# Weight parts interleaved element by element, paired activations, and streams read backward, in a float32 decoder layer on one core

## The chip, the cores and the metric

The kernel runs on one core of one Trainium2 chip. The metric is the device time of one execution in microseconds (us). Before the change it is 1109.9 us, the median of two runs (1109.86 and 1109.95). TensorE (PE in the profile) multiplies: it loads a 128 x 128 block (the stationary operand; the loads are shown as PEld) and streams columns past it (the moving operand). VectorE is DVE, ScalarE is ACT, GpSimd is POOL and SyncE is SP; SP issues the loads of weights.

## The reference

One decoder layer in float32, 256 tokens, width 2048. What matters here is its four weight products:

```
h = rms_norm(x, ln_mix_pre)
proj = h @ w_in                                   # 2048 x 5648
mixed = concat([attn, ssm]) @ w_out               # 2048 x 2048
x = x + rms_norm(mixed, ln_mix_post)
h = rms_norm(x, ln_ffn_pre)
u = causal_depthwise_conv(h @ w_ffn_up)           # 2048 x 11264
gate, up = split(u)
f = (gelu(gate, approximate=True) * up) @ w_ffn_down   # 5632 x 2048
x = x + rms_norm(f, ln_ffn_post)
```

Attention (8 heads) and the state-space mixer (16 heads) work on the 256 tokens between the first two products.

## The kernel before, in words

**Split operands.** Every operand of the four products is split into two parts, hi (the value rounded to fp32r) and lo (the rest). A product is hi·hi + lo·hi + hi·lo. Activations are split once; weights are split on the fly.

**Units of weights.** Weights come in units of 128 x 1024 elements (512 KB), in the order in which they are used: 88 of the input projection, 32 of the output projection, and twice 88 of the up and 44 of the down projection. `Weights.rounded` handles one unit: SP loads it into `raw` (L77), ACT writes `whi` (L78), DVE writes `wlo` (L79). `raw` has four slots. `whi` and `wlo` have four slots each, as separate tiles, and seven from the output projection on (`deepen`). Whenever TensorE has used a unit, `tick` fetches the next one for which there is a slot.

**Two forms of product.** In the *column* form (`cols_part`, L214 and L215; input projection in part, and up) the weights are stationary: a 128 x 128 slice of hi is loaded and both parts of the activations are streamed (512 columns), then the slice of lo is loaded and the hi activations are streamed (256 columns). A unit holds eight such pairs, and two units make one tile of 128 output columns. In the *row* form (`rows_part`, L278 to L280; the rest of the input projection, output and down) the activations are stationary and 512 columns of weights are streamed, three matmuls per slice, twelve per unit.

**The activations.** `hT` (input) and `mT` (output projection's input) hold the hi and lo parts of a slice of 128 rows one behind the other; `h2` (up) holds them as two planes; `gT` (down) is like `mT`. Up and down run in two halves of 22 slices each. An index `i` of the up loop makes one tile of the gate and one of the up branch; after it `cols_sum` adds the two column groups in PSUM (ACT L231, DVE L232), `conv_ffn` and `gated` apply the convolution, the gelu and the product, and `split_evac` (L201, L202) writes slice `i` of `gT`.

**What sets the order.** TensorE's order is that of the program; ACT's and DVE's are made by a scheduler from the program and its dependences, except around the second norm, where it is written by hand.

Of the kernel before, what the change touches and what calls it, by code (L numbers as in the profile page):

```python
# [19 lines left out]
P = 128  # L20
D = 2048
S = 256
# [18 lines left out]
LOE = UE + 2 * SHIFT  # L41
HOLD = 5
MORE = {"raw": 0, "whi": 3, "wlo": 3}
# [15 lines left out]
class Weights:  # L59

    def __init__(self, nc, pool, units):
        self.nc, self.pool, self.units = nc, pool, units
        self.fetched, self.ready, self.more, self.base, self.behind = 0, [], None, 0, 0

    def deepen(self, pool):

        self.more, self.base, self.behind = pool, self.fetched, MORE["whi"]

# [11 lines left out]
    def place(self, i, n, bufs, dtype):  # L82
        pool = self.pool
        if self.more and (i - self.base) % (bufs + MORE[n]) < MORE[n]:
            pool, bufs = self.more, MORE[n]
        wide = n == "wlo" and pool is self.pool
        return pool.tile([P, LOE if wide else UE], dtype, name=n, tag=n, bufs=bufs)
# [36 lines left out]
def decoder_layer(ctx, tc, x, xT, win, wdt, wout, wup, wdown, relb, vec, cols, mconv, fconv,  # L124
# [85 lines left out]
    def cols_part(ps, w, aT, k, j):  # L210

        s = tok(j)
        both, hi, c = wide_and_hi(aT, k)
        nc.tensor.matmul(ps, w[0][:, s], both, start=(k == 0), stop=False)  # L214
# [14 lines left out]
    def cols_sum(dst, ps):  # L229

        nc.scalar.copy(dst, ps[:, S:])  # L231
        nc.vector.tensor_tensor(dst, ps[:, :S], dst, op=ALU.add)  # L232
# [17 lines left out]
    def cols_tile(ps, aT):  # L250
        for u in range(2):
            w = ws.take()
            for j in range(8):
                cols_part(ps, w, aT, u * 8 + j, j)
# [57 lines left out]
    def units(w, a, n, shift=0):  # L312
        return [(w[i], shift) for i in range(a, a + n)]
# [4 lines left out]
                    for u in units(wup, half * 88, 88) + units(wdown, half * 44, 44)])  # L318
# [32 lines left out]
    def summands(aT):  # L351

        if len(aT.shape) == 4:
# [591 lines left out]
    gT = fp.tile([P, HALF, 2, S], F32R, name="gT")  # L945
# [5 lines left out]
    def summed(ps):  # L951
        u = fp.tile([P, S], F32, name="cfu", tag="cf", bufs=8)
        cols_sum(u, ps)
# [51 lines left out]
    def gated(i, ug, uu):  # L1005
# [5 lines left out]
        split_evac(gT, k, slice(0, S), cu)  # L1011
# [134 lines left out]
```

## Time and profile before

| | |
|---|---|
| median of two runs | 1109.9 us |
| profiled execution, first to last instruction | 1107.4 us |
| around it (median less span) | 2.5 us |
| mean granted TensorE clock | 0.998 |
| busy: PE / DVE / ACT | 99% / 71% / 53% |
| moved by DMA | 217.58 MB, mean 196 GB/s |

The page gives no time of its own for the profiled execution beside its span, so the 2.5 us are the median less the span. A busy PE is not a TensorE at its peak, since ends of matmuls are modelled; the pace at which matmuls start is what counts. In groups of instructions the last columns are the busy time, the mean of one in ns, the idle time of the engine before them, and what ended it. In rows by stage each engine has its busy time and, in brackets, its number of instructions.

### The profile page before, as it was taken

The numbers are of one execution on the slowest core, as the hardware profiler recorded it, in microseconds if no ns is written. First come the engines' busy times: TensorE is split into PE (matmuls) and PEld (weight loads), VectorE is DVE, ScalarE is ACT, GpSimd is POOL, SyncE is SP. The second block draws the span as 40 slices with busy tenths as digits, with TensorE's granted clock in tenths as the row PEclk, the third lists the DMA queues.
The fourth block names the chain that finished last, engine by engine and source line by source line (L and its number), as shares of the span: only waits on it lengthen the run. The fifth ranks groups of instructions, "written<-read, shape, count | busy, mean of one in ns | idle before, by whom it ended". The sixth has DMA issues, their size and how long they took to land.

```text
span 1107.4 us, 15791 instructions
## 1 busy us (share of the span) xinstructions
PE 1100.1 (99%) x5888; PEld 945.1 (85%) x5888; DVE 784.0 (71%) x1270; ACT 592.3 (53%) x914; POOL 15.5 (1%) x26
## 2 busy tenths in 40 slices
PE   9999999999999999999999999999999999999997
PEld 7888888888888988888888888888888888888886
DVE  6698976776566899878787644448787878765553
ACT  6666545545454586555555444345555555554441
POOL 0010000000000000000000000000000000000000
PEclk9999999999999999999999999999999999999999
DMA  8857555555687267665556665565566565666652
GB/s 297 298 187 262 186 154 167 177 172 168 217 298 245 96 216 242 192 189 190 191 188 189 194 195 190 192 194 188 191 189 191 189 192 190 189 201 219 200 158 76
DMA packets 61356, 217.58 MB, mean 196 GB/s; under 512 B 7200, under 2 KB 8624, under 8 KB 60384
## 3 DMA queue, kind: packets, MB, share of 16 engines
q1 hardware_dynamic: 59328, 207.64, 58.3%
q0 software_dynamic: 1664, 8.59, 2.3%
q8 instruction: 46, 0.75, 0.3%
q10 hardware_dynamic: 288, 0.35, 0.1%
q14 instruction: 30, 0.25, 0.1%
HBM read 214.44 MB, written 2.11 MB: 196 GB/s over the span
## 4 chain that ended last, share of the span: by engine, by line
PE 99%; DMA 0%; SPq 0%; ACT 0%; issue 0%; DVE 0%; POOLq 0%; ACTq 0%
PE pa L214 36%; PE pa L215 18%; PE pa L278 9%; PE pa L280 9%; PE pa L279 9%; PE ph L280 4%; PE ph L279 4%; PE ph L278 4%; PE pab L214 1%; PE pa L223 1%; PE pab L215 1%; PE py L604 1%; PE pa L226 0%; PE pq L223 0%; DMA raw<-in_win_dram 0%; PE lg L694 0%
## 5 line engine op out<-in xcount | busy, mean ns | idle before, releaser
L79 DVE TENSOR_TENSOR wlo<-raw,whi 128x1024 fp32r<-128x1024 f32 (+2 forms) x389 | 469.7, 1210 | 249.0 <-ACT whi L78 240.9
L78 ACT CAST whi<-raw 128x1024 fp32r<-128x1024 f32 (+2 forms) x389 | 403.7, 1040 | 415.5 <-PE pa L214 193.3
L214 PE MATMUL pa<-h,whi 128*128 128x512 f32 x1360 | 471.7, 394 | 0.0
L215 PE MATMUL pa<-h,wlo 128*128 128x256 f32 x1360 | 379.4, 279 | 0.0
L214 PEld LDWEIGHTS pa<-h,whi 128*128 128x128 f32 x1360 | 255.7, 188 | 57.7
L215 PEld LDWEIGHTS pa<-h,wlo 128*128 128x128 f32 x1360 | 255.5, 188 | 0.0
L214 PE MATMUL pa<-hT,whi 128*128 128x512 f32 x384 | 136.5, 397 | 0.0
L215 PE MATMUL pa<-hT,wlo 128*128 128x256 f32 x384 | 107.0, 281 | 0.0
L214 PEld LDWEIGHTS pa<-hT,whi 128*128 128x128 f32 x384 | 72.1, 188 | 15.2 <-issue 0.2
L962 DVE SCALAR_TENSOR_TENSOR cfc<-cfu,fcv,cfc 128x254 f32<-128x254 f32 (+1 forms) x176 | 83.5, 479 | 1.4
L215 PEld LDWEIGHTS pa<-hT,wlo 128*128 128x128 f32 x384 | 72.1, 189 | 0.6 <-issue 0.2
L278 PE MATMUL pa<-whi,gT 128*128 128x512 f32 x176 | 68.6, 390 | 0.0
L280 PE MATMUL pa<-whi,gT 128*128 128x512 f32 x176 | 68.5, 389 | 0.0
L278 PE MATMUL ph<-whi,gT 128*128 128x512 f32 x176 | 68.5, 389 | 0.0
L279 PE MATMUL pa<-wlo,gT 128*128 128x512 f32 x176 | 68.5, 389 | 0.0
L279 PE MATMUL ph<-wlo,gT 128*128 128x512 f32 x176 | 68.5, 389 | 0.0
L280 PE MATMUL ph<-whi,gT 128*128 128x512 f32 x176 | 68.5, 389 | 0.0
L960 ACT ACTIVATE cfc<-cfu,fcv 128x256 f32<-128x256 f32 x88 | 52.3, 598 | 1.3 <-DVE cfu L959 1.3
L278 PE MATMUL pa<-whi,hT 128*128 128x512 f32 x128 | 51.2, 400 | 0.0
L278 PE MATMUL pa<-whi,mT 128*128 128x512 f32 x128 | 50.3, 393 | 0.0
L280 PE MATMUL pa<-whi,hT 128*128 128x512 f32 x128 | 50.1, 392 | 0.0
L279 PE MATMUL pa<-wlo,hT 128*128 128x512 f32 x128 | 50.0, 391 | 0.0
(230 smaller groups left out, 1131.6 us busy)
## 6 DMA issues: line engine op xcount, KB each, us to landing
raw<-in_wup_dram SPq DMA_DIRECT2D x176, 512.0 KB, 3.7
raw<-in_wdown_dram SPq DMA_DIRECT2D x88, 512.0 KB, 3.6
raw<-in_win_dram SPq DMA_DIRECT2D x85, 512.0 KB, 3.6
raw<-in_wout_dram SPq DMA_DIRECT2D x32, 512.0 KB, 3.9
xsq<-in_x_dram SPq DMA_DIRECT2D x2, 1024.0 KB, 10.3
rows<-acd POOLq DMA_DIRECT2D x4, 512.0 KB, 8.9
xt<-in_x_dram POOLq DMA_DIRECT2D x2, 1024.0 KB, 6.7
xr<-in_xT_dram SPq DMA_DIRECT2D x6, 256.0 KB, 6.4
```

What stands on the lines that cost most here:

```text
L78: nc.scalar.copy(hi[:, s], raw[:, s])
L79: return lambda: nc.vector.tensor_tensor(lo[:, s], raw[:, s], f32(hi[:, s]), op=ALU.subtract)
L214: nc.tensor.matmul(ps, w[0][:, s], both, start=(k == 0), stop=False)
L215: end[0] = nc.tensor.matmul(ps[:, c], w[1][:, s], hi, start=False, stop=(k == KT - 1)).ins
L223: nc.tensor.matmul(both, w[0][:, s], aT[:, :, c:c + S][:, :, tok(t)], start=(t == 0 and k == 0), stop=False)
L278: nc.tensor.matmul(ps, a, w[0][:, s], start=(first and j == 0), stop=False)
L279: nc.tensor.matmul(ps, a, w[1][:, s], start=False, stop=False)
L280: end[0] = nc.tensor.matmul(ps, b, w[0][:, s], start=False, stop=(last and j == 1)).ins
L604: nc.tensor.matmul(py[:, i * 64:(i + 1) * 64], rows[:, t, g, i, :], xcs[t, g][:, i * 64:(i + 1) * 64], start=True, stop=True)
L960: nc.scalar.activation(c, u, AF.Identity, scale=wv[:, 2:3], bias=wv[:, 3:4])
L962: nc.vector.scalar_tensor_tensor(c[:, sh:], u[:, :S - sh], wv[:, 2 - sh:3 - sh], c[:, sh:], op0=ALU.mult, op1=ALU.add)
```

## The change

The two parts of a unit of weights now lie in one tile `wx`, with as many slots as before (four, and seven after `deepen`). A unit has one of three layouts. *plane*: hi in the first 1024 elements, lo in the next. *pair*: hi and lo alternate element by element, so that a slice of either is read and written at every second element. *plane-*: as plane, but each part is written backward, and the matmuls read it backward.

- Up: of the index `i`, `i % 4` in 0 and 1 is plane, 2 and 3 is pair. The start of a pair unit is shifted by 0, 16, 32 or 48 elements with `i // 4 % 4`, where the slot has room. For odd `i` above 1 the streamed `h2` is read backward (`back`), and `cols_sum` reads PSUM backward to put the columns right.
- Output projection: `mT` holds hi and lo element by element; they are the stationary operand.
- Down: weights in layout plane-, so the stream is read backward in both halves. `gT` stays in planes in the first half and is paired in the second.
- Input projection: layouts plane, and nothing is read backward.

```
-MORE = {"raw": 0, "whi": 3, "wlo": 3}
+MORE = 3
...
+    def place(self, i):
+        if self.more and (i - self.base) % (SPLB + MORE) < MORE:
+            return self.more.tile([P, 2 * UE], F32R, name="wx", tag="wx", bufs=MORE), 0
+        return self.pool.tile([P, 2 * UE + 2 * SHIFT], F32R, name="wx", tag="wx", bufs=SPLB), 1
...
-        raw = self.place(i, "raw", RAWB, F32)
-        hi, lo = (self.place(i, n, SPLB, F32R) for n in ("whi", "wlo"))
-        lo = lo[:, self.units[i][1]:][:, :UE]
+        raw = self.pool.tile([P, UE], F32, name="raw", tag="raw", bufs=RAWB)
+        w, room = self.place(i)
+        _, layout, shift = self.units[i]
+        if layout[:4] == "pair":
+            w = w[:, shift * room:][:, :2 * UE]
+            hi, lo = (w.rearrange("p (c z) -> p z c", z=2)[:, z, :] for z in range(2))
+        else:
+            hi, lo = w[:, :UE], w[:, UE + shift:][:, :UE]
+        if layout[-1] == "-":
+            hi, lo = hi[:, ::-1], lo[:, ::-1]
...
-    def cols_part(ps, w, aT, k, j):
+    def cols_part(ps, w, aT, k, j, back=False):
         s = tok(j)
         both, hi, c = wide_and_hi(aT, k)
+        if back:
+            both, hi = both[:, :, ::-1], hi[:, ::-1]
...
+    def cols_sum(dst, ps, back=False):
+        a, b = ps[:, S:], ps[:, :S]
+        if back:
+            a, b = a[:, ::-1], b[:, ::-1]
+        nc.scalar.copy(dst, a)
+        nc.vector.tensor_tensor(dst, b, dst, op=ALU.add)
...
+    layouts = ["plane", "plane", "pair", "pair"]
+    def up_units(i):
+        return units(wup, 4 * i, 4, 16 * (i // 4 % 4) if i % 4 > 1 else 0, layouts[i % 4])
...
-                    for u in units(wup, half * 88, 88) + units(wdown, half * 44, 44)])
+                    for u in [u for i in range(22 * half, 22 * half + 22) for u in up_units(i)]
+                    + units(wdown, half * 44, 44, 0, "plane-")])
...
-        mT = mx.tile([P, KT, 2, S], F32R, name="mT")
+        mT = mx.tile([P, KT, S, 2], F32R, name="mT")
+        mT = tuple(mT[:, :, :, c] for c in range(2))
...
-    gT = fp.tile([P, HALF, 2, S], F32R, name="gT")
+    gTs = fp.tile([P, HALF, 2 * S], F32R, name="gT")
+    gT = [tuple(gTs[:, :, c * S:(c + 1) * S] for c in range(2)),
+          tuple(gTs.rearrange("p k (s c) -> p k c s", c=2)[:, :, c, :] for c in range(2))]
...
+            back = i > 1 and i % 2 == 1
...
-                cols_tile(ps[-1], h2)
-            us = [summed(p) for p in ps]
+                cols_tile(ps[-1], h2, back)
+            us = [summed(p, back) for p in ps]
```

TensorE's instructions stand in the same order as before, and so do SP's and POOL's. ACT's and DVE's order moves, since the two parts share a tile. On DVE, in the first up stage, from the last step of one index to the splits of the next (`cfu` and `cfc` are an up tile and its convolution, `pa` is PSUM, L79 is the split of a unit), before:

```order
L202 TENSOR_TENSOR gT_3837<-cfc_4363,gT_3837 128x256
L232 TENSOR_TENSOR cfu_4461<-pa_4371,cfu_4461 128x256
L959 TENSOR_TENSOR cfu_4461<-cfu_4461,rb2_3841 128x256
L79 TENSOR_TENSOR wlo_4457<-raw_4455,whi_4456 128x1024
L79 TENSOR_TENSOR wlo_4500<-raw_4498,whi_4499 128x1024
L232 TENSOR_TENSOR cfu_4464<-pa_4416,cfu_4464 128x256
L962 SCALAR_TENSOR_TENSOR cfc_4467<-cfu_4461,fcv_3838,cfc_4467 128x255
L959 TENSOR_TENSOR cfu_4464<-cfu_4464,rb2_3841 128x256
L962 SCALAR_TENSOR_TENSOR cfc_4467<-cfu_4461,fcv_3838,cfc_4467 128x254
L79 TENSOR_TENSOR wlo_4522<-raw_4520,whi_4521 128x1024
```

The same place on DVE in the changed kernel (L81 is the split, L244 the sum out of PSUM, L982 and L985 the convolution):

```order
L209 TENSOR_TENSOR gT_3705<-cfc_4319,gT_3705 128x256
L244 TENSOR_TENSOR cfu_4413<-pa_4327,cfu_4413 128x256
L982 TENSOR_TENSOR cfu_4413<-cfu_4413,rb2_3709 128x256
L81 TENSOR_TENSOR wx_4409<-raw_4408,wx_4409 128x1024
L244 TENSOR_TENSOR cfu_4416<-pa_4370,cfu_4416 128x256
L982 TENSOR_TENSOR cfu_4416<-cfu_4416,rb2_3709 128x256
L985 SCALAR_TENSOR_TENSOR cfc_4419<-cfu_4413,fcv_3706,cfc_4419 128x255
L985 SCALAR_TENSOR_TENSOR cfc_4419<-cfu_4413,fcv_3706,cfc_4419 128x254
L81 TENSOR_TENSOR wx_4451<-raw_4450,wx_4451 128x1024
```

The sum of the second tile (L232, now L244) has moved ahead of the second split. On ACT, at the same place, before (L78 writes hi, L231 copies out of PSUM):

```order
L231 COPY cfu_4461<-pa_4371 128x256
L78 CAST whi_4456<-raw_4455 128x1024
L78 CAST whi_4499<-raw_4498 128x1024
L231 COPY cfu_4464<-pa_4416 128x256
L960 ACTIVATE cfc_4467<-cfu_4461,fcv_3838 128x256
L78 CAST whi_4521<-raw_4520 128x1024
```

And on ACT in the changed kernel (L80 writes hi, L243 copies out of PSUM):

```order
L243 COPY cfu_4413<-pa_4327 128x256
L80 CAST wx_4409<-raw_4408 128x1024
L243 COPY cfu_4416<-pa_4370 128x256
L983 ACTIVATE cfc_4419<-cfu_4413,fcv_3706 128x256
L80 CAST wx_4451<-raw_4450 128x1024
```

The copy of the second tile has moved ahead of the second cast.

More of the change, by code (lines that the diff above doesn't have):

```diff
@@ L67, in deepen @@
     def deepen(self, pool):
-        self.more, self.base, self.behind = pool, self.fetched, MORE["whi"]
+        self.more, self.base, self.behind = pool, self.fetched, MORE
     def split(self, raw, hi, lo, i, s):
@@ L80, in rounded @@
                                                op=ALU.subtract)
[L82 to L87, printed above, removed]
-    def tiles(self, i):
-        raw = self.place(i, "raw", RAWB, F32)
-        hi, lo = (self.place(i, n, SPLB, F32R) for n in ("whi", "wlo"))
-        lo = lo[:, self.units[i][1]:][:, :UE]
+    def place(self, i):
+        if self.more and (i - self.base) % (SPLB + MORE) < MORE:
+            return self.more.tile([P, 2 * UE], F32R, name="wx", tag="wx", bufs=MORE), 0
+        return self.pool.tile([P, 2 * UE + 2 * SHIFT], F32R, name="wx", tag="wx", bufs=SPLB), 1
+    def tiles(self, i):
+        raw = self.pool.tile([P, UE], F32, name="raw", tag="raw", bufs=RAWB)
[8 more added lines that the diff above has]
+            hi, lo = hi[:, ::-1], lo[:, ::-1]
         self.ready.append((hi, lo))
@@ L248, in tick, with cols_tile @@
                 fn(*args)
-    def cols_tile(ps, aT):
+    def cols_tile(ps, aT, back=False):
         for u in range(2):
@@ L253, in cols_tile @@
             for j in range(8):
-                cols_part(ps, w, aT, u * 8 + j, j)
+                cols_part(ps, w, aT, u * 8 + j, j, back)
             tick()
@@ L310, in rows_tail, with units @@
         rows_part(pss[t], tail[j], aT, kts[len(kts) - HOLD + j], t, False, j == HOLD - 1)
-    def units(w, a, n, shift=0):
-        return [(w[i], shift) for i in range(a, a + n)]
+    def units(w, a, n, shift=0, layout="plane"):
+        return [(w[i], layout, shift) for i in range(a, a + n)]
+    layouts = ["plane", "plane", "pair", "pair"]
+    def up_units(i):
+        return units(wup, 4 * i, 4, 16 * (i // 4 % 4) if i % 4 > 1 else 0, layouts[i % 4])
     ws = Weights(nc, wp, units(win, 0, 16, SHIFT) + units(win, 16, 16) + units(win, 32, 16, SHIFT)
@@ L351, in summands @@
     def summands(aT):
+        if isinstance(aT, tuple):
+            return aT
         if len(aT.shape) == 4:
@@ L949, in decoder_layer, with summed @@
     rb2 = pers.tile([P, S], F32, name="rb2", tag="rbc", bufs=1)
-    def summed(ps):
+    def summed(ps, back):
         u = fp.tile([P, S], F32, name="cfu", tag="cf", bufs=8)
-        cols_sum(u, ps)
+        cols_sum(u, ps, back)
         return u
@@ L1010, in gated @@
         nc.vector.tensor_tensor(cu, cg, cu, op=ALU.mult)
[L1011 removed]
+        split_evac(gT[i // HALF], k, slice(0, S), cu)
     held = []
@@ L1032, in decoder_layer @@
                 held.append([psum("ph") for _ in range(NT)])
-                rows_chunk(held[-1], gT, range(0, HALF, 2), last=False)
+                rows_chunk(held[-1], gT[half], range(0, HALF, 2), last=False)
             elif half == 1 and c == 2:
-                rows_chunk(held[0], gT, range(0, HALF, 2), first=False, done=fdone(1, c))
+                rows_chunk(held[0], gT[half], range(0, HALF, 2), first=False, done=fdone(1, c))
             elif half == 1 and c == 3:
@@ L1038, in decoder_layer @@
                 kts = range(0, HALF, 2)
-                tail = rows_to_tail(held[1], gT, kts, first=False)
+                tail = rows_to_tail(held[1], gT[half], kts, first=False)
                 for t in range(NT):
                     for j in range(HOLD):
-                        rows_tail(held[1], gT, kts, tail, t, j)
+                        rows_tail(held[1], gT[half], kts, tail, t, j)
                     fdone(1, 3)(t, held[1][t])
             else:
-                rows_chunk(chunk_psums(), gT, range(0, HALF, 2), done=fdone(half, c))
+                rows_chunk(chunk_psums(), gT[half], range(0, HALF, 2), done=fdone(half, c))
 def _cols_units(w):
```

4 lines of the change are left out of this document (removed).

## The prediction

> **What bounds the kernel now.** I read the page's busy times and its chain of waits first, then the stages one by one.
>
> ```profile
> PE 1100.1 (99%) x5888; PEld 945.1 (85%) x5888; DVE 784.0 (71%) x1270; ACT 592.3 (53%) x914; POOL 15.5 (1%) x26
> ...
> PE 99%; DMA 0%; SPq 0%; ACT 0%; issue 0%; DVE 0%; POOLq 0%; ACTq 0%
> PE pa L214 36%; PE pa L215 18%; PE pa L278 9%; PE pa L280 9%; PE pa L279 9%; PE ph L280 4%; PE ph L279 4%; PE ph L278 4%; PE pab L214 1%; PE pa L223 1%; PE pab L215 1%; PE py L604 1%; PE pa L226 0%; PE pq L223 0%; DMA raw<-in_win_dram 0%; PE lg L694 0%
> ```
>
> The chain that ends last is TensorE for 99% of the span; no other engine and no transfer has a whole percent of it. So the time is the number of matmuls times the pace at which TensorE starts them. Ends of matmuls are modelled (each is shown some 0.17 us longer than the step to the next), so I take the pace from counts in stages: the first up stage, the first down, the second up, the second down, and the output projection.
>
> ```profile
> core 0: us, PE busy (x) PEld busy (x) DVE busy (x) ACT busy (x) POOL busy (x), PEclk, DMA share, GB/s
> 390.00:610.00 220.00, 220.00 (x1271) 193.09 (x1270) 181.15 (x300) 135.30 (x215) 0.72 (x1) 1.00 0.62 199
> 625.00:725.00 100.00, 100.00 (x443) 82.86 (x442) 45.17 (x37) 40.73 (x41) 0.00 (x0) 1.00 0.61 194
> 760.00:970.00 210.00, 210.00 (x1213) 184.28 (x1212) 165.62 (x265) 122.11 (x190) 0.00 (x0) 1.00 0.60 189
> 985.00:1085.00 100.00, 100.00 (x442) 82.83 (x442) 51.53 (x53) 43.71 (x50) 0.00 (x0) 1.00 0.55 182
> 300.00:360.00 60.00, 60.00 (x267) 49.68 (x265) 40.26 (x47) 29.11 (x36) 0.00 (x0) 1.00 0.81 282
> ```
>
> The granted clock is 1.00 throughout. One matmul of each count only overlaps an edge. In the up stage 1270 matmuls, 635 pairs of a 512-column one (L214) and a 256-column one (L215), take 220 us: 0.3465 us a pair, and 210/606 = 0.3465 in the second half. In the down stage every matmul streams 512 columns: 100/442 = 0.2262 us each (0.2268 and 0.2256 in the other two rows).
>
> Two paces give two unknowns, p per column and q per matmul with the weight load that goes with each: 512p + q = 226.2 ns and 768p + 2q = 346.5 ns. Twice the first less the second is 256p = 105.9, so p = 0.414 ns and q = 14.4 ns. This q is what TensorE loses around each load, and the only part of the pace that a layout can take away.
>
> Check: 1856 pairs x 0.3465 + 1824 row matmuls x 0.2262 = 643 + 413 = 1056 us; the other 51 us of the span are the start, the mixers' small matmuls and the tail. The span is 1107.4 us and the median 1109.9, so 2.5 us lie around it; I add the change to 1109.9.
>
> **The change part by part.** No matmul is added, removed or moved on TensorE. What changes is how 3488 of them read memory:
> - Up, half of the tiles: 704 pairs load weights at every second element (1408 loads).
> - Up, odd tiles after the first: 672 pairs stream h backward, 352 of them among the 704, 320 with contiguous weights.
> - Output projection: 384 matmuls load paired mT; the stream stays forward.
> - Down: 1056 matmuls stream weights backward, and the 528 of the second half also load paired gT.
>
> So 2320 loads become strided and 2400 streams run backward. Input projection, and 384 up pairs, keep their reads.
>
> *A strided load.* The trace has none; how near a load is to setting the pace can be read where the stream is short, and how long loads are shown in the up stage:
>
> ```profile
> 122.86 1.73 PE py L604 x16
> ...
> L214 PEld LDWEIGHTS pa<-h,whi x1360: 187/188/189, 387.6 to 978.7; 128*128 128x128 f32 x195
> L214 PE MATMUL pa<-h,whi x1360: 388/395/476, 387.7 to 978.8; 128*128 128x512 f32 x195
> ```
>
> Sixteen 64-column matmuls, each with its own load, take 1.73 us: 108 ns each, so a load occupies about 108 ns. The 256-column step has 346.5 − 226.2 = 120 ns for one: a load may grow by only 12 ns before it shows there; under 512 columns it has 118 ns to spare. I bound a strided load's effect on its matmul by −14.4 ns (q disappears) below and +96 ns above, the second only in the 704 up pairs (load doubled to 216 ns against 120). Nearest is the load as it stands, so I take 0: the same 128 elements per partition, no row that shows address or offset changing q as a whole. The offsets do show in the split of it:
>
> ```profile
> start us, us, engine line op out<-in xcount [idle before <-releaser]
> ...
> 451.04 0.39 PE L214 MATMUL pa<-h,whi 128*128 128x512 f32 x1
> ...
> 451.38 0.40 PE L214 MATMUL pa<-h,whi 128*128 128x512 f32 x1
> ...
> 451.73 0.39 PE L214 MATMUL pa<-h,whi 128*128 128x512 f32 x1
> ...
> 452.07 0.40 PE L214 MATMUL pa<-h,whi 128*128 128x512 f32 x1
> ...
> 452.43 0.39 PE L214 MATMUL pa<-h,whi 128*128 128x512 f32 x1
> ```
>
> Successive pairs take 0.34, 0.35, 0.34 and 0.36 us: a short and a long one in turn, as the slices' addresses alternate, with 0.347 as their mean. Addresses matter by about 7 ns a pair either way, and it evens out.
>
> The Trainium skill speaks for 0 here: "SBUF — State Buffer", section Specifications (TRN2), gives 16-byte lines that need at least two hits each for full bandwidth, and a paired fp32 load has exactly two. No run here shows that. The same line says that each new line pays a penalty, which is the first rival below.
>
> *A backward stream.* TensorE reads nothing backward in this trace. Other engines do, and write forward:
>
> ```profile
> L733 DVE SCALAR_TENSOR_TENSOR qT<-kT,rbc 128x256 f32<-128x256 f32 x8 | 3.4, 426 | 0.2
> L738 DVE TENSOR_TENSOR kT<-kT,rbc 128x256 f32<-128x256 f32 x8 | 3.4, 426 | 0.2
> L202 DVE TENSOR_TENSOR mT<-pav,mT 128x256 fp32r<-128x256 f32 x8 | 3.3, 416 | 0.0
> L202 DVE TENSOR_TENSOR gT<-cfc,gT 128x256 fp32r<-128x256 f32 x44 | 18.4, 419 | 4.9 <-ACT gT L201 4.8
> ```
>
> L733 reads both inputs backward and takes 426 ns, as L738 does forward; L202 reads PSUM backward in 416 ns against 419 forward. So direction costs these nothing, and I take 0 for TensorE and for the reversed sums after the up tiles. Bounds: q gone or doubled in 2400 matmuls, ±35 us.
>
> *Writing the new layouts.* The splits write at every second element in 88 up units, and backward in the 88 down units.
>
> ```profile
> L79 DVE TENSOR_TENSOR wlo<-raw,whi 128x1024 fp32r<-128x1024 f32 x381 | 465.4, 1224 | 247.2 <-ACT whi L78 239.2
> L79 DVE TENSOR_TENSOR wlo<-raw,whi 128x512 fp32r<-128x512 f32 x4 | 2.8, 692 | 1.4 <-ACT whi L78 1.4
> L78 ACT CAST whi<-raw 128x1024 fp32r<-128x1024 f32 x381 | 399.7, 1051 | 413.6 <-PE pa L214 193.3 <-PE pa L280 83.9 <-PE ph L280 57.5
> ```
>
> Per element DVE takes (1224 − 692)/512 = 1.04 ns. An up unit is eight pairs, 2.77 us; 220 us hold 79.4 of them, so DVE works 181.15/79.4 = 2.28 us a unit and ACT 1.70. Unchanged writes cost 0. If a strided write took two beats per element, DVE would need 2.28 + 1.06 = 3.35 us in paired units, 0.58 over; the mean with plain units is 2.81 against 2.77, so 0.04 x 176 = 7 us; without the slots' lead to even it out, 0.58 x 88 = 51 us. The cover is that lead: L78 mostly idles until TensorE frees a slot, so seven slots (19 us) stay filled, more than the 8 x 0.58 = 4.6 us that a run of paired units would draw. ACT, at 1.70 + 0.86, stays under 2.77; the down units have DVE busy only 45%.
>
> *One tile for both parts.* A slot is now free only when hi and lo are both read: one matmul, up to 0.23 us, later; it comes out of the same 19 us. TensorE's waits per unit stay one on ACT and one on DVE. In the moved order the second PSUM sum comes ahead of a split (1.22 us) instead of behind it; that frees PSUM earlier, and the chain shows nobody waiting there. Sum: 0, so 1110 us.
>
> **The rivals.**
> 1. *The toll doubles on strided loads.* A paired load spans 1024 bytes instead of 512. If q is paid per stretch of memory read and not per load, each of 2320 loads costs 14.4 ns more: +33 us, 1143 us, slower. For it: q exists though a load (108 ns) fits under every stream, so the two disturb each other. Against it: the pairs above at alternating addresses keep the mean. It decides from +9.6 ns a load (22 us). A rule in "TensorE: Matmul & The Clock Gate", section Step-by-step, would exclude it: stream and loads have separate read ports. That page's gap of N/2.4 + 2.5 ns is 216 ns for 512 columns; the trace has 226, so it does not agree fully here.
> 2. *Strided loads take twice as long.* 216 ns against the 120 ns step: +96 ns x 704 = 68 us, 1178 us; row matmuls hide it (216 < 226). Nothing speaks for it but the missing row.
> 3. *Load and stream stop meeting.* A plain load walks 512 bytes in 108 ns, 4.7 bytes/ns, the stream 4/0.414 = 9.7; a paired load walks 9.5, in step with a forward stream. If q comes from the two crossing, it goes in the 704 forward paired matmuls and the 384 of the output projection: −16 us, 1094; if in all 2320, −33 us, 1077.
> 4. *DVE becomes the bound* through strided writes: +7 to +51 us, 1117 to 1161.
> 5. *Backward streams lose pace*: up to +35 us or more, from 1145.
>
> **How the numbers follow.** No change in pace, within some 10 us: 0.56. Rival 1: 0.16 (0.12 of it beyond 2%), rival 2: 0.06, rival 3: 0.15 (0.09 beyond 2%), rival 4: 0.04 (half of it), rival 5: 0.03. Two per cent is 22 us, about what a measurement of this kernel can tell from no change. Faster 0.09, same 0.56 + 0.04 + 0.06 + 0.02 = 0.68, slower 0.12 + 0.06 + 0.02 + 0.03 = 0.23. The range takes in rival 3 short of its end and rival 1 to its end: 1080 to 1144; outside lie rivals 2 and 5, part of 4 and the ends of 1 and 3, about 0.18.
>
> **What would show it.** The up stage at 0.3465 us a pair in all four kinds of tile and the down stage at 0.226 confirm it. Pairs of 0.375 in paired tiles are rival 1, 0.44 with longer load records rival 2, 0.32 rival 3. Idle time of PE ended by DVE in the up stage is rival 4, with L81 over 2 us. A down stage whose two halves differ prices paired gT alone; both moving together prices the backward stream.

## The result and the profile after

The changed kernel takes 1125.49 us (1125.47 to 1125.50) against 1109.9 us before: a ratio of 1.0137, 95% interval 1.0107 to 1.0166. It is slower by 15.6 us. That is inside the predicted range and below the 2% bound, but the interval leaves no room for "nothing happened": the predicted size, 0, was wrong. The spans of the two profiled executions differ by 16.2 us, 1123.6 against 1107.4.

The page's busy times and the chain of waits of the changed kernel are these:

```profile
PE 1116.2 (99%) x5888; PEld 960.3 (85%) x5888; DVE 785.2 (70%) x1270; ACT 599.5 (53%) x914; POOL 15.6 (1%) x26
...
PE 99%; DMA 0%; SPq 0%; ACT 0%; issue 0%; DVE 0%; POOLq 0%; ACTq 0%
```

The chain is TensorE's for 99%, as before. No engine took its place and no wait was added. DVE has 785.2 us of work (784.0 before), and ACT's 7 us more are not on the chain. So TensorE itself starts its matmuls more slowly. Where it does is seen in the rows by stage, in this order: heads and input projection, output projection, first up stage, first down, second up, second down. The figures in brackets behind the PE and PEld times are numbers of matmuls and of loads.

```profile
core 0: us, PE busy (x) PEld busy (x) DVE busy (x) ACT busy (x) POOL busy (x), PEclk, DMA share, GB/s
120.00:300.00 180.00, 180.00 (x987) 155.67 (x986) 128.23 (x244) 91.03 (x167) 5.51 (x8) 1.00 0.54 168
300.00:360.00 60.00, 60.00 (x259) 49.63 (x258) 40.20 (x47) 29.83 (x37) 0.00 (x0) 1.00 0.81 280
395.00:620.00 225.00, 225.00 (x1283) 198.39 (x1282) 182.73 (x303) 138.57 (x214) 0.72 (x1) 1.00 0.63 196
630.00:730.00 100.00, 100.00 (x431) 80.55 (x430) 44.13 (x36) 39.47 (x40) 0.00 (x0) 1.00 0.61 189
775.00:980.00 205.00, 205.00 (x1167) 180.72 (x1166) 159.71 (x256) 120.05 (x181) 0.00 (x0) 1.00 0.62 188
1000.00:1090.00 90.00, 90.00 (x387) 76.01 (x386) 47.22 (x48) 40.50 (x47) 0.00 (x0) 1.00 0.61 194
```

Before, the first down stage held 442 matmuls in 100 us and the output projection 266 in 60 us, one fewer than counted, since one only overlaps an edge; now they hold 430 and 258. A row matmul of the down stage takes 100/430 = 0.2326 us instead of 0.2262, and a pair of the up stage 225/641 = 0.3510 us instead of 0.3465. The first row, where only the shared tile and the order of the work changed, holds 987 matmuls, and held 988 before. The granted clock is 1.00 in every row. The sum over a window blurs the edges, so below I also use the mean step from one matmul's start to the next one's start in the same trace: 226.7 ns for every row matmul of the down stage before, 233.3 ns for every one after, in both halves, with over 9 in 10 of them within 1.5 ns of that.

In the up stage the four kinds of tile follow one another, 32 pairs each. These are the starts of the first 512-column matmul of the indices 28 (plane, forward), 29 (plane, backward), 30 (paired, forward), 31 (paired, backward) and 32, from the timeline of TensorE:

```profile
start us, us, engine line op out<-in xcount [idle before <-releaser]
...
811.79 0.40 PE L223 MATMUL pa<-h,wx 128*128 128x512 f32 x1
...
822.88 0.40 PE L223 MATMUL pa<-h,wx 128*128 128x512 f32 x1
...
834.20 0.40 PE L223 MATMUL pa<-h,wx 128*128 128x512 f32 x1
...
845.48 0.40 PE L223 MATMUL pa<-h,wx 128*128 128x512 f32 x1
...
856.79 0.40 PE L223 MATMUL pa<-h,wx 128*128 128x512 f32 x1
```

The differences are 11.09, 11.32, 11.28 and 11.31 us: 0.3466 us a pair where nothing was touched, as before, and 0.3525 to 0.3537 in the three other kinds. A backward stream, a paired load and both together cost the same 6 to 7 ns a pair.

What was to cost nothing on DVE and ACT, and the loads of one line, L290, as grouped by what they load:

```profile
L81 DVE TENSOR_TENSOR wx<-raw,wx 128x1024 fp32r<-128x1024 f32 x381 | 465.3, 1223 | 228.3 <-ACT wx L80 227.3
L80 ACT CAST wx<-raw 128x1024 fp32r<-128x1024 f32 x381 | 407.3, 1071 | 354.5 <-PE pa L224 125.2 <-PE pa L292 91.5 <-PE ph L292 60.0
...
L290 PEld LDWEIGHTS pa<-wx,hT x128: 186/188/192, 52.4 to 201.6; 128*128 128x128 f32 x128
L290 PEld LDWEIGHTS pa<-wx,mT x128: 193/193/198, 277.3 to 369.6; 128*128 128x128 f32 x128
L290 PEld LDWEIGHTS pa<-wx,gT x176: 188/192/197, 620.9 to 1052.5; 128*128 128x128 f32 x176
```

DVE's split takes 1223 ns (1224 before), ACT's cast 1071 (1051) in the mean over all units. A load from paired data is recorded at 193 ns in the median against 188 for a contiguous one: 5 ns, not the doubling of rival 2.

The account closes. Of the row matmuls, 384 in the output projection and 1056 in the down stages were touched: 1440 x 6.6 = 9.5 us. Of the up pairs, 320 plane-backward, 352 paired-forward and 352 paired-backward, some 1024 x 6.7 = 6.9 us. Together 16.4 us; the spans differ by 16.2.

### The profile page after: what moved, and what is told of

It is laid out like the page before. It is cut to its first block, busy times and chain, and to the rows that moved or that the text cites. A ratio compares the mean times of both kernels' runs of the same rounds, so it can differ in the third digit from the quotient of the medians.

```text
span 1123.6 us, 15775 instructions
## 1 busy us (share of the span) xinstructions
PE 1116.2 (99%) x5888; PEld 960.3 (85%) x5888; DVE 785.2 (70%) x1270; ACT 599.5 (53%) x914; POOL 15.6 (1%) x26
## 4 chain that ended last, share of the span: by engine, by line
PE 99%; DMA 0%; SPq 0%; ACT 0%; issue 0%; DVE 0%; POOLq 0%; ACTq 0%
PE pa L223 36%; PE pa L224 18%; PE pa L290 9%; PE pa L292 9%; PE pa L291 9%; PE ph L290 4%; PE ph L292 4%; PE ph L291 4%; PE pab L223 1%; PE pa L232 1%; PE pab L224 1%; PE py L625 1%; DMA raw<-in_win_dram 0%; PE pa L235 0%; PE pq L232 0%; PE lg L715 0%
## 5 line engine op out<-in xcount | busy, mean ns | idle before, releaser
L81 DVE TENSOR_TENSOR wx<-raw,wx 128x1024 fp32r<-128x1024 f32 (+2 forms) x389 | 469.6, 1210 | 230.2 <-ACT wx L80 229.1
L80 ACT CAST wx<-raw 128x1024 fp32r<-128x1024 f32 (+2 forms) x389 | 411.3, 1059 | 356.5 <-PE pa L224 125.2
L223 PE MATMUL pa<-h,wx 128*128 128x512 f32 x1360 | 478.4, 398 | 0.0
L224 PE MATMUL pa<-h,wx 128*128 128x256 f32 x1360 | 381.0, 280 | 0.0
L223 PEld LDWEIGHTS pa<-h,wx 128*128 128x128 f32 x1360 | 260.7, 192 | 56.4
L224 PEld LDWEIGHTS pa<-h,wx 128*128 128x128 f32 x1360 | 261.9, 193 | 0.0
L223 PE MATMUL pa<-hT,wx 128*128 128x512 f32 x384 | 136.6, 398 | 0.0
L224 PE MATMUL pa<-hT,wx 128*128 128x256 f32 x384 | 106.9, 280 | 0.0
L985 DVE SCALAR_TENSOR_TENSOR cfc<-cfu,fcv,cfc 128x254 f32<-128x254 f32 (+1 forms) x176 | 83.7, 480 | 2.9
L223 PEld LDWEIGHTS pa<-hT,wx 128*128 128x128 f32 x384 | 72.2, 188 | 15.4 <-issue 0.2
L224 PEld LDWEIGHTS pa<-hT,wx 128*128 128x128 f32 x384 | 72.1, 189 | 0.4 <-issue 0.2
L290 PE MATMUL pa<-wx,gT 128*128 128x512 f32 x176 | 69.9, 397 | 0.0
L292 PE MATMUL pa<-wx,gT 128*128 128x512 f32 x176 | 69.9, 397 | 0.0
L290 PE MATMUL ph<-wx,gT 128*128 128x512 f32 x176 | 69.9, 397 | 0.0
L291 PE MATMUL ph<-wx,gT 128*128 128x512 f32 x176 | 69.9, 397 | 0.0
L292 PE MATMUL ph<-wx,gT 128*128 128x512 f32 x176 | 69.9, 397 | 0.0
L291 PE MATMUL pa<-wx,gT 128*128 128x512 f32 x176 | 69.9, 397 | 0.0
L243 ACT COPY cfu<-pa 128x256 f32<-128x256 f32 x87 | 31.9, 368 | 67.1 <-PE pa L224 67.1
L244 DVE TENSOR_TENSOR cfu<-pa,cfu 128x256 f32<-128x256 f32 x87 | 36.4, 420 | 33.9 <-ACT cfu L243 33.9
L290 PE MATMUL pa<-wx,hT 128*128 128x512 f32 x128 | 51.2, 400 | 0.0
L290 PE MATMUL pa<-wx,mT 128*128 128x512 f32 x128 | 50.9, 398 | 0.0
```

The costliest lines, as they stand in the source:

```text
L80: nc.scalar.copy(hi[:, s], raw[:, s])
L81: return lambda: nc.vector.tensor_tensor(lo[:, s], raw[:, s], f32(hi[:, s]), op=ALU.subtract)
L224: end[0] = nc.tensor.matmul(ps[:, c], w[1][:, s], hi, start=False, stop=(k == KT - 1)).ins
L243: nc.scalar.copy(dst, a)
L244: nc.vector.tensor_tensor(dst, b, dst, op=ALU.add)
L290: nc.tensor.matmul(ps, a, w[0][:, s], start=(first and j == 0), stop=False)
```

## The experiments

All kernels start from the changed one with one common edit: the layouts and directions come from tables, one entry for each up index and each quarter of a down stage, and the stationary operands `mT` and `gT` from a helper that gives a slice's two parts side by side (`pair`) or one behind the other (`flat`). The diffs show, in short form, the entries that differ: of the first kernel and of the two that undo one cause against the changed kernel, of the others against the first. The kernel with paired weights at another start is shown against the one with paired weights alone. A time without an interval is that of a single run, the profiled one.

**All reads put back, the rest of the change kept.** This separates what TensorE reads from the shared tile `wx`, the order on DVE and ACT, and the new addresses.

```diff
-    layouts = ["plane", "plane", "pair", "pair"]
+    layouts = ["plane", "plane", "plane", "plane"]
-    units(wdown, half * 44, 44, 0, "plane-")
+    units(wdown, half * 44, 44, 0, "plane")
-        mT = tuple(mT[:, :, :, c] for c in range(2))
+        mT = stationary(mT, KT, "flat")
+    gT = [stationary(gTs, HALF, w) for w in ['flat', 'flat']]
-            back = i > 1 and i % 2 == 1
+            back = False
```

> hi and lo share one tile as in the change, but every unit is plane and read forward, mT and gT lie in planes. Theory A (the cost is the way TensorE reads: one step of about 6.7 ns for each 512-column matmul whose load is strided or whose stream runs backward): the down stage at 0.2265 us a matmul, up pairs at 0.3465 us, 1109.9 us. Theory B (the cost is the shared tile: new addresses, later slot release, moved order on ACT and DVE): some or all of the 15.6 us stay, up to 1125 us.

Measured: 1109.51 us, ratio 0.9996 (0.9987 to 1.0005). The two down stages by the same view:

```profile
630.00:730.00 100.00, 100.00 (x443) 82.81 (x442) 45.33 (x37) 40.90 (x41) 0.00 (x0) 1.00 0.62 193
1000.00:1090.00 90.00, 90.00 (x399) 74.53 (x398) 44.50 (x45) 35.64 (x43) 0.00 (x0) 1.00 0.51 163
```

442 matmuls in 100 us again. The shared tile, the later release of a slot and the moved order are worth nothing that can be measured; the 15.6 us lie in how TensorE reads, or in the strided and backward writes that went with it, for which the count above leaves nothing. This kernel, with a span of 1107.9 us, is the base for the next three.

**Paired activations alone.** `mT` and both halves of `gT` paired, everything streamed forward, weights in planes.

```diff
-        mT = stationary(mT, KT, "flat")
-    gT = [stationary(gTs, HALF, w) for w in ['flat', 'flat']]
+        mT = stationary(mT, KT, "pair")
+    gT = [stationary(gTs, HALF, w) for w in ['pair', 'pair']]
```

> As the run with the shared tile alone, and mT and gT (both halves) are paired; all streams run forward. Theory A: 384 + 1056 row matmuls at 0.2333 instead of 0.2267 us, +9.6 us, 1119.5 us; the up stage unchanged. Rival A2 (a strided load costs only where it is read against a forward stream of the output projection, and in the down stage the direction alone was paid): down at 0.2267, only +2.6 us, 1112.5 us.

Measured: 1119.17 us, ratio 1.0082 (1.0069 to 1.0096), against 1119.5 expected of the access pattern itself.

```profile
630.00:730.00 100.00, 100.00 (x430) 82.74 (x429) 44.07 (x36) 39.45 (x40) 0.00 (x0) 1.00 0.61 190
1000.00:1090.00 90.00, 90.00 (x387) 74.43 (x387) 45.70 (x46) 37.98 (x45) 0.00 (x0) 1.00 0.59 183
```

Both down stages go at 0.233 us with every stream forward. So a load at every second element costs its row matmul 6.6 ns, although the load has 118 ns to spare under the stream.

**Backward streams alone.** The odd up tiles after the first and both down stages backward; all loads contiguous.

```diff
-    UP = [("plane", False, 0) ...]
-    DOWN = [["plane"] * 4, ["plane"] * 4]
+    UP = [("plane", i > 1 and i % 2 == 1, 0) for i in range(44)]
+    DOWN = [["plane-"] * 4, ["plane-"] * 4]
```

> As the run with the shared tile alone, and the streams run backward as in the change (odd up tiles after the first, both down halves); no element is interleaved. Theory A: 1056 row matmuls at 0.2333 (+7.0 us) and 672 up pairs at 0.3534 instead of 0.3467 us (+4.5 us), 1121.4 us. Rival A2, additive costs: half of a step each, about 1115 us.

Measured: 1121.53 us, ratio 1.0103 (1.0089 to 1.0117), against 1121.4 expected.

```profile
630.00:730.00 100.00, 100.00 (x430) 80.55 (x430) 44.13 (x36) 39.32 (x40) 0.00 (x0) 1.00 0.60 190
1000.00:1090.00 90.00, 90.00 (x388) 72.50 (x387) 46.87 (x48) 37.98 (x45) 0.00 (x0) 1.00 0.58 187
```

The same counts to within one: a backward stream costs as much as a paired load. The backward pairs take 353.4 ns where the forward ones of the same kernel take 346.7.

**Paired weights alone.** Half of the up tiles paired with the change's shifts, all streams forward.

```diff
-    UP = [("plane", False, 0) ...]
+    UP = [(layouts[i % 4], False, 16 * (i // 4 % 4) if i % 4 > 1 else 0) for i in range(44)]
```

> As the run with the shared tile alone, and half of the up tiles have paired weights with the shifts of the change; all streams run forward, mT and gT in planes. Theory A: 704 up pairs at 0.3535 instead of 0.3467 us, +4.8 us, 1114.7 us; L81 and L80 on DVE and ACT keep 1.23 and 1.05 us. Rival: the pairs with a strided load cost nothing where the stream runs forward, 1109.9 us.

Measured: 1114.18 us, ratio 1.0035 (1.0021 to 1.0049), against 1114.7 expected; 353.1 ns a paired pair in the mean, 352.3 to 353.3 by shift.

The three parts are worth 9.2, 11.6 and 4.4 us of span over the base, 25.2 together. The change, which has all three (with `gT` paired in one half only), is worth 15.7 over it. For that one half, 528 x 6.6 ns = 3.5 us come off the sum, which leaves 21.7. The 528 down matmuls and 352 up pairs that have two of the three then account for the other 6 us: 528 x 6.6 + 352 x 6.7 ns = 5.8 us. So where a matmul has two of them, it pays once. Two runs test that directly for the down stage.

**One of two causes taken out of the second down stage.** First the changed kernel with `gT` in planes there (backward stays), then with that stage streamed forward (paired `gT` stays).

```diff
-    gT = [flat, pair]
+    gT = [flat, flat]
```

> The change with gT in planes in the second half too (the weights are still streamed backward there). Theory D (one step a matmul, not adding): nothing is won, 1125.5 us. Rival (each departure has a cost of its own): half of the step on 528 matmuls comes back, 1123.7 us or less.

```diff
-    DOWN = [["plane-"] * 4, ["plane-"] * 4]
+    DOWN = [["plane-"] * 4, ["plane"] * 4]
```

> The change with the weights of the second down half streamed forward (gT stays paired there). Theory D: nothing is won, 1125.5 us; the matmuls stay at 0.2333. Rival: 1123.7 us or less.

Measured: 1125.78 us, ratio 1.0139 (1.0124 to 1.0154), and 1125.39 us, ratio 1.0136 (1.0119 to 1.0153); the changed kernel's own ratio is 1.0137. The second down stage of the first and of the second:

```profile
1000.00:1090.00 90.00, 90.00 (x387) 72.54 (x386) 47.20 (x48) 40.38 (x47) 0.00 (x0) 1.00 0.60 193
```

```profile
1000.00:1090.00 90.00, 90.00 (x387) 74.64 (x386) 47.22 (x48) 40.62 (x48) 0.00 (x0) 1.00 0.60 191
```

386 loads in 90 us in both, and in the changed kernel. Undoing either cause wins nothing while the other stays: one step of 6.6 ns, not two.

**Wider strides.** Is it paid for each line of memory that a load touches? `mT` and the first half's `gT` lie with two slices' parts side by side, so that a load reads every fourth element; the second half's `gT` is paired. In each down stage the weights of the last two column blocks are paired, so that there it is the stream that reads every second element. All up tiles but two are paired.

```diff
-    DOWN = [["plane"] * 4, ["plane"] * 4]
+    DOWN = [["plane", "plane", "pair", "pair"], ["plane", "plane", "pair", "pair"]]
-        mT = stationary(mT, KT, "flat")
-    gT = [stationary(gTs, HALF, w) for w in ['flat', 'flat']]
+        mT = stationary(mT, KT, "quad")
+    gT = [stationary(gTs, HALF, w) for w in ['quad', 'pair']]
```

> mT, and gT in the first half, lie with hi and lo of two slices side by side, so that a load reads every fourth element (16 bytes apart); gT in the second half is paired (8 bytes apart). The weights are plane and forward in the first two blocks of 512 columns of each down half and paired in the last two, so that the stream reads every second element there. All up tiles but the first two are paired, odd ones streamed backward, half of them started 16 elements later. Theory C (the loss grows with the number of 16-byte lines that a load touches: 13 ns for 32 lines, 20 for 64): 128 lines give at least 33 ns, so 0.246 us a row matmul in the output projection and the first down half, +0.0195 us against plain. Theory D (one step, whatever departs from forward and contiguous): 0.2333 there too. A load that takes twice its time stays hidden under 0.227 us. A stream at every second element: 0.2333 by D and by the two-elements-to-a-line rule; 0.44 us if lines set the stream's pace.

Measured: 1246.16 us, a single run. By stage: first half with the stream contiguous, then with the stream at every second element; second half likewise.

```profile
625.00:670.00 45.00, 45.00 (x194) 45.00 (x193) 22.13 (x23) 19.82 (x22) 0.00 (x0) 1.00 0.59 187
720.00:800.00 80.00, 80.00 (x177) 55.00 (x176) 18.30 (x15) 15.57 (x14) 0.00 (x0) 1.00 0.30 96
1060.00:1100.00 40.00, 40.00 (x173) 33.08 (x172) 20.23 (x21) 18.45 (x21) 0.00 (x0) 1.00 0.63 210
1150.00:1230.00 80.00, 80.00 (x178) 37.77 (x177) 18.06 (x24) 12.06 (x16) 0.56 (x1) 1.00 0.16 53
```

With the stream contiguous, loads at every fourth element leave 45/193 = 0.233 us a row matmul, like those at every second (40/172 = 0.233); by starts, which do not blur at the window's edges, 235.0 and 233.3 ns. At least 246 was expected if each line touched had its price, so that theory falls. And the load itself did get longer here: the first row has loads recorded from end to end (45.00 us of 45.00), and L312's are

```profile
L312 PEld LDWEIGHTS pa<-wx,gT x65: 308/310/311, 624.9 to 670.0; 128*128 128x128 f32 x65
```

310 ns at every fourth element, against 193 at every second and 188 contiguous. A load 122 ns longer in the record adds 2 ns to the step. Whether these 235 ns come of the pattern or of the length stays open: the sixteen short matmuls from which the prediction took its 108 ns a load start 112 ns apart, and 112 + 122 = 234 ns, an estimate of what such a load occupies, is as long as the step.

The other two rows were not foreseen: with the *stream* at every second element a row matmul takes 80/176 = 0.455 and 80/177 = 0.452 us, twice 0.2267. The Trainium skill, "SBUF — State Buffer", section Specifications (TRN2), gives full bandwidth to an access with two hits in each 16-byte line, and these have two. For the loads the trace agrees (193 against 188 ns, and 310 where one hit is left), and for DVE's writes as well: its split at every second element takes 1224 ns as before. The writes of `gT` at every fourth element, in the first half, take 638 and 676 ns where the changed kernel's, half of them paired, take 420 and 416. In the rows of this run's engines from 390 to 640 us:

```profile
L231 DVE TENSOR_TENSOR gT<-cfc,gT 128x256 fp32r<-128x256 f32 x22 | 13.9, 638 | 0.9 <-ACT gT L230 0.9
L230 ACT CAST gT<-cfc 128x256 fp32r<-128x256 f32 x22 | 14.6, 676 | 1.9 <-DVE cfc L1055 1.9
```

ACT's cast of a unit, which takes 1051 ns in the kernel before, takes 1143 in the mean here, where most units are paired, so its writes are not free at every second element. For TensorE's stream the trace does not agree: it reads two elements of each line and still goes at half the pace.

**The same reads at other addresses.** Everything contiguous, but `gT`'s slices lie 532 elements apart instead of 512, so that loads start at many places of a stretch of 64 elements; the up weights start 0 to 60 elements later where the slot has room. First down stage forward, second backward.

```diff
-    gTs = fp.tile([P, HALF * 2 * S], F32R, name="gT")
+    GP = 2 * S + 20
+    gTs = fp.tile([P, HALF * GP], F32R, name="gT")
-    UP = [("plane", False, 0) ...]
-    DOWN = [["plane"] * 4, ["plane"] * 4]
+    UP = [("both" if i < 22 else "over", False, 4 * i % 64) for i in range(44)]
+    # both: hi and lo start later; over: lo alone; tiles 0 and 1 as before
+    DOWN = [["plane"] * 4, ["plane-"] * 4]
```

> Shared tile, everything plane and contiguous, but starts differ: slices of gT lie 532 elements apart instead of 512, so that loads start at all multiples of 16 bytes within 256 bytes; weights of up tiles start 0 to 60 elements later (both parts in the first half, only lo in the second; only in the slots that have room). First down half forward, second backward. Theory E (the loss depends on where load and stream stand to each other in memory): the forward row matmuls spread, some at 0.220 or less and some at 0.233 or more, and some backward ones come back to 0.2267; up pairs spread likewise. Theory D (the pattern alone): 0.2267 forward and 0.2333 backward at all starts, up pairs 0.3467 on the mean.

Measured: 1118.18 us, a single run.

```profile
630.00:730.00 100.00, 100.00 (x433) 81.03 (x433) 43.98 (x37) 39.91 (x40) 0.00 (x0) 1.00 0.61 189
1000.00:1090.00 90.00, 90.00 (x386) 72.23 (x385) 45.81 (x47) 37.49 (x44) 0.00 (x0) 1.00 0.56 179
```

Forward, contiguous and still 433 instead of 443: row matmuls of 226 to 241 ns by start address, 231.8 in the mean. Backward ones had 231 to 240, 234.2 in the mean, none back at 227. Neither theory holds as stated: the starts matter, but none goes below 226. Up pairs, contiguous and forward, took 347 to 355 ns by their start address. So 226.7 is not the pace of a contiguous read as such; it belongs to the regular places at which the kernel's slices lie. Most of the step can be had without any stride or direction.

**The same for paired loads.** `gT` paired and 532 elements apart, first down stage forward, second backward; all up tiles but two paired, with starts 0 to 60, forward in the first half.

```diff
-    UP = [("plane", False, 0) ...]
-    DOWN = [["plane"] * 4, ["plane"] * 4]
+    UP = [("pair", i > 21, 4 * i % 64) for i in range(44)]  # tiles 0 and 1 as before
+    DOWN = [["plane"] * 4, ["plane-"] * 4]
-    gT = [flat at 512, flat at 512]
+    gT = [pair at 532, pair at 532]
-        mT = stationary(mT, KT, "flat")
+        mT = stationary(mT, KT, "pair")
```

> As the run of offsets, with paired loads: gT paired in both halves, its slices 532 elements apart, stream forward in the first half and backward in the second; all up tiles but two paired with starts 0 to 60 elements later in the slots that have room, forward in the first half, backward in the second. Theory E (where load and stream stand to each other decides): some starts give 0.2267 us a row matmul and 0.3467 us an up pair with paired loads too. Theory D (the pattern decides): no start does; all means lie at 0.233 to 0.236 and at 0.350 to 0.355.

Measured: 1126.94 us, a single run; rows 232.0 ns in the mean forward (226 to 240 by start address), 233.7 backward. In the up stage, forward, two places stand out in the timeline: pairs whose two parts start at elements 24 and 25 of a stretch of 64, and at 32 and 33. Of each the fence has two starts with 15 pairs between them.

```profile
start us, us, engine line op out<-in xcount [idle before <-releaser]
...
424.48 0.40 PE L245 MATMUL pa<-h,wx 128*128 128x512 f32 x1
...
429.88 0.40 PE L245 MATMUL pa<-h,wx 128*128 128x512 f32 x1
...
445.07 0.39 PE L245 MATMUL pa<-h,wx 128*128 128x512 f32 x1
...
450.27 0.39 PE L245 MATMUL pa<-h,wx 128*128 128x512 f32 x1
```

5.40/15 = 0.360 us a pair at the first, 5.20/15 = 0.347 at the second: the pace of an untouched pair, with paired weights. The other fourteen starts lie between (350 to 356 ns in the mean), and backward pairs take 350.0 to 354.4 ns by their start address, never less.

**Paired weights, at the good start.** If the start is what counts, the cost of pairing should go with a shift alone. 600 of the 704 paired pairs now start 32 elements into their stretch of 64, the others at 40, for which the three later slots became 32 elements larger; what lies behind them in memory moved with that.

```diff
+AT = (24, 24, 0)
-            return self.more.tile([P, 2 * UE], ...), 0
+            return self.more.tile([P, 2 * UE + SHIFT], ...), 0
-            w = w[:, shift * room:][:, :2 * UE]
+            at = 24 if room else AT[(i - self.base) % (SPLB + MORE)]
+            w = w[:, at:][:, :2 * UE]
-        pad(..., "pad2", 48)
+        pad(..., "pad2", 16)
```

> As the run with paired weights alone (half of the up tiles, all streams forward), but 600 of the 704 paired slices' pairs start 128 bytes into a 256-byte stretch instead of 32, and 104 start 160 bytes into one. In the run of paired offsets those starts took 0.3470 and 0.3502 us a pair, against 0.3534 at 32. Theory E (the start decides): paired tiles at 0.347 to 0.348 us, 1110.3 us, the cost of pairing gone. Theory D (the pattern decides): 0.3534, 1114.2 us as before.

Measured: 1114.03 us, ratio 1.0035 (1.0021 to 1.0049), the same as with the change's shifts. The pairs did get better where they should: 349.5 ns in the mean at 32 (347 in the median, 343 to 357), 356.4 at 40. But the row matmuls lost:

```profile
630.00:730.00 100.00, 100.00 (x441) 82.42 (x440) 45.10 (x37) 40.51 (x41) 0.00 (x0) 1.00 0.60 194
```

440 loads in 100 us instead of 442, 227.7 ns by the steps between starts instead of 226.7: about 1 ns on each of 1056 down matmuls, 1.1 us, against some 3 x 600 − 3 x 104 = 1.5 us won in the pairs (at 353 ns before the shift). The rows lost it in the units of one slot in seven (232.7 ns) and in those right after them (227.9); the others stay at 226.7. What moved one read to a better place moved another to a worse one.

The start is part of the cost and not all of it. The fence has, for the indices 3 and 10, the time at which the first of 16 pairs starts and that at which the pair behind them does. By the rotation of the seven slots, both times the weights lie in the same slots, start at 32 and are read against the same slices of `h2`:

```profile
start us, us, engine line op out<-in xcount [idle before <-releaser]
...
408.62 0.39 PE L247 MATMUL pa<-h,wx 128*128 128x512 f32 x1
...
414.22 0.39 PE L247 MATMUL pa<-h,wx 128*128 128x512 f32 x1
...
486.48 0.39 PE L247 MATMUL pa<-h,wx 128*128 128x512 f32 x1
...
492.03 0.39 PE L247 MATMUL pa<-h,wx 128*128 128x512 f32 x1
```

They take 5.60/16 = 0.350 us a pair (343 and 357 ns in turn) and 5.55/16 = 0.347. Shortly before the first 16 a unit that starts at 40 had been read, before the second 16 none since the last contiguous tile. Nine of the eleven stretches of paired tiles have such a unit inside. From the second unit behind it they go at 350 ns a pair; ahead of it eight go at about 347, and the ninth, the first of the second up stage, at 350 or more. So what ran just before seems to carry over into the pace; no run was made to test that.

**Paired `gT` at other starts, and contiguous weights read against a backward stream.**

```diff
-    gT = [flat, flat]
+    gT = [pair at 24, pair at 12]       # first slices then lie 32 and 20 elements into a stretch of 64
-    UP = [("plane", False, 0) ...]
+    UP = [("both", True, 4 * i % 64) for i in range(44)]  # 0 and 1 as before
```

> Paired gT read against forward streams, starting 128 bytes into a 256-byte stretch in the first down half and 80 in the second (32 in the change); all up tiles but two with contiguous weights that start 0 to 60 elements later where there is room, and h streamed backward. Theory E: some of these starts bring the paired row matmuls back towards 0.2267 us and some backward up pairs back towards 0.3467. If it is the start only for forward streams (as the runs of offsets suggest), paired rows move and backward pairs stay at 0.350 to 0.3535.

Measured: 1124.19 us, a single run.

```profile
630.00:730.00 100.00, 100.00 (x430) 84.02 (x429) 43.77 (x36) 39.50 (x40) 0.00 (x0) 1.00 0.59 189
1000.00:1090.00 90.00, 90.00 (x391) 76.47 (x390) 47.21 (x48) 41.19 (x48) 0.00 (x0) 1.00 0.60 193
```

At 32 the rows stay at 233.4 ns, at 20 they go to 231.1: 2.2 ns of the 6.6 come back. The good start of the up weights is not a good start for `gT`. Backward pairs take 350 to 355 ns at the sixteen starts, 350.0 at best. No start that was tried brings a backward stream to 346.7.

**Narrower loads.** Does the step grow with what is loaded? In the down stages the inner matmuls load 64 columns instead of 128, which leaves out the products of half of the tokens; the blocks alternate between forward and backward streams, and the second half's `gT` is paired.

```diff
+            if first and j == 0 or last and j == 1:
+                n = P
+            ps_, a, b = (ps, a, b) if n == P else (ps[:n], a[:, :n], b[:, :n])
-    DOWN = [["plane"] * 4, ["plane"] * 4]
+    DOWN = [["plane", "plane-", "plane", "plane-"], ["plane", "plane-", "plane", "plane-"]]
-    gT = [flat, flat]
+    gT = [flat, pair]
```

> In the down stage all matmuls but the first and last unit of each block load 64 columns instead of 128 (half of the tokens' products are left out, so the output is not the layer's); gT is in planes in the first half and paired in the second; the blocks' streams run forward and backward in turn. Theory C (loss per line or per element loaded): half the loss, 0.220 us forward and contiguous, and 0.2267 paired (64 columns touch as many lines as 128 contiguous ones). Theory F (loss per matmul, whatever the load): 0.2267 and 0.2333 as with 128 columns.

Measured: 1114.97 us, a single run. By block: contiguous forward, contiguous backward, then paired forward, paired backward.

```profile
616.00:646.00 30.00, 30.00 (x132) 18.76 (x131) 16.45 (x19) 13.70 (x17) 0.00 (x0) 1.00 0.63 193
648.00:675.00 27.00, 27.00 (x118) 16.02 (x117) 11.73 (x11) 10.46 (x10) 0.00 (x0) 1.00 0.60 181
...
982.00:1010.00 28.00, 28.00 (x122) 17.31 (x121) 15.27 (x18) 14.26 (x17) 0.58 (x1) 1.00 0.68 226
1012.00:1040.00 28.00, 28.00 (x122) 17.15 (x121) 14.51 (x14) 11.85 (x14) 0.00 (x0) 1.00 0.60 188
```

Such short windows err by one or two matmuls at their edges, so here I go by the steps between starts: 230.0, 233.3, 231.7 and 233.3 ns, against 30/131 = 0.229, 27/117 = 0.231 and twice 28/121 = 0.231 by the counts. Half the load does not halve the loss. The contiguous forward block even became slower than with full loads (226.7), and the backward one did not move. A price for each column loaded is out.

## Why the prediction was right, and where it was wrong

**The range: held, in part by luck.** The forecast was 1110 us, and two terms that it took as 0, below, make up the 15.6 us. The measured 1125.5 lies between 1080 and 1144 because the range was opened upward for rival 1, whose mechanism the runs refute; the backward streams, which alone cost 11.6 us, had been placed outside it.

**The bound: right.** TensorE still has 99% of the chain, at a granted clock of 1.00, and the whole difference is the pace of its matmuls.

**Writing, one tile, the moved order, reversed sums: 0, and right.** DVE's split is 1223 ns against 1224, ACT's 20 ns longer beside the path, the sums out of PSUM, half of them reversed, take 420 ns on DVE (418 before), and with the reads put back the time is 0.9996 of before. The 16.4 us counted on TensorE's reads alone leave nothing for the writes.

**A strided load: taken as 0, measured +6.6 ns for a row matmul and 6 to 7 for a pair.** This is the first of the two mis-sized terms. It lies within the stated bounds (−14.4 to +96 ns), and much nearer to the low end. The working had the loss q around each load as something that a layout either leaves or takes away. It can also raise it, by 6.6/14.4 = 46% for a row matmul.

**A backward stream: taken as 0, measured +6.6 to 6.7 ns.** The second term. The rows that it was taken from are DVE's, and they said nothing about TensorE. The bound of one q (14.4 ns) held.

**The row that did price it was quoted and read past.** Successive pairs of the kernel before took 0.34 and 0.35 to 0.36 us in turn; by starts, 340 and 354 ns for alternate slices; the loaded and the streamed slice both alternate, and no run separates them. I wrote that this evens out. It does as long as half of the pairs have the good place; the backward pairs all take 353.4 ns, the longer of the two. The 7 ns that I set aside as the spread were the size of the step to come: 2464 matmuls and pairs x 6.65 = 16.4 us, against 0 in the sum.

**Rival 1 (the toll doubles on strided loads): right in sign and place, under half in price, wrong in mechanism.** 6.6 ns instead of 14.4, and not paid for each stretch of memory read: loads over twice the stretch of the paired ones add 2 ns, not 14.4 or more.

**Rival 2 (loads take twice as long): out.** Paired loads are recorded at 193 ns against 188. Where loads were recorded at 310 ns, the rows hid it but for 2 ns over the paired ones.

**Rival 3 (load and stream in step): out.** Pairing with a forward stream was to win 14.4 ns; it lost 6.6, and at the best start it only reached the pace of before.

**Rival 4 (DVE): out.** DVE has no whole percent of the chain, and the splits are no longer.

**Rival 5 (backward streams lose pace): right in kind, at 0.03 too unlikely, and a third of its price**: 11.6 us for the backward streams alone, not 35.

**The test that the prediction set itself was too weak.** It said that both down halves moving together prices the backward stream. They did, and it does; but paired `gT` alone gives the very same pace, and undoing either leaves 0.233. A signature that reads two causes from one pace holds only if they add up.

**What stays open.** Stride, direction and start of the access each move the pace, and the first two not on top of each other; at one and the same start address the pace took two values. That fits a collision of the load's reads with the stream's, from which the kernel's regular places had been partly free; but no run shows the collision itself. The Trainium skill, "TensorE: Matmul & The Clock Gate", section Step-by-step, has stream and loads on separate read ports, so that loading the next weights takes no read bandwidth from the running matmul; here the layout of what is loaded sets the pace, 233.3 against 226.7 ns with the stream untouched, so the trace does not agree in full. Whether a load read back to front would meet a backward stream as the forward ones meet was not tried, and how long a matmul without a load beside it takes was not measured either. None of the kernels beats the one before.

## What to carry to other kernels

Where TensorE sets the pace back to back, the way in which its two operands lie is worth a per cent or more: keep stationary operands contiguous and streams forward, do not expect that to be enough at irregular starts (231.8 ns here against 226.7), and compare the mean step of each kind of matmul, kind by kind, before and after a change of layout. Do not let a stream of this type read every second element: it took twice as long, where a load cost 6.6 ns and DVE's writes nothing. Prices of access patterns need not add, so undo each cause with the others in place before putting a price on it.

## What the runs showed that was not expected

- A stream at every second fp32 element goes at half the pace: 453 to 455 ns for 512 columns against 226.7. A load at every second element costs 6.6 ns, at every fourth 8.
- Stride and direction cost the same step, 226.7 to 233.3 ns, and only once.
- Loads at irregular starts cost contiguous forward matmuls 5 ns (231.8 ns in the mean); paired pairs run from 347 to 360 ns by their start address, and at one address took 347 or 350 ns, as it seems by what ran before them.
- A load recorded at 310 ns instead of 188 costs the 227 ns step of its matmul 8 ns, while halving the columns of a contiguous load makes the matmul 3 ns slower.
- Writes of 256 elements at every fourth element took DVE 638 ns instead of 419 and ACT 676 instead of 406 (the kernel before); at every second one DVE's take 421 and ACT's 428.
